# A spacer tile of 96 instead of 32 bytes at the right end of the on-chip memory of a hybrid decoder layer

## The chip, the cores and the metric

The kernel runs on one core of one Trainium2 chip. The metric is the device time of one execution in microseconds (us), as a median of three runs.

## The reference

One decoder layer on x of 1024 tokens by 1024 channels, in float32, in three steps. Each step normalises its input and scales and shifts it by vectors worked out from a condition c (`w_ada`).

```python
def swiglu(h, w12, w3):
    a, b = jnp.split(h @ w12, 2, axis=-1)
    return (jax.nn.silu(a) * b) @ w3
...
x = x + 0.5 * (1.0 + gate[:, 0, None]) * swiglu(h, ffn1_w12[l], ffn1_w3[l])
...
x = x + (1.0 + gate[:, 1, None]) * token_mix(h, w_in[l], ...)
...
x = x + 0.5 * (1.0 + gate[:, 2, None]) * swiglu(h, ffn2_w12[l], ffn2_w3[l])
```

The inner width of both feed-forward blocks is 2816. `token_mix` runs a differential attention and an mLSTM, four heads each, side by side, and ends in a projection by `w_out`. The two feed-forward blocks do the same arithmetic on different weights.

## The kernel before

**Products.** Every large product is kept at float32 precision by splitting both factors in a high and a low part of type float32r: `mm3` (L196 to L200) issues three matmuls of 128 x 128 weights by 128 x 512 moving elements: high by high (L198), high by low (L199), low by high (L200). In the names of the profile, whi and wlo are the parts of a weight tile, the weights of a matmul; what stands before them (B11h, B22l, S, ghi, glo, k) is its moving operand.

```python
def mm3(self, ps, whi, wlo, xhi, xlo, first, last):
    nc = self.nc
    nc.tensor.matmul(ps, whi, xhi, start=first, stop=False, skip_group_check=True)
    nc.tensor.matmul(ps, whi, xlo, start=False, stop=False, skip_group_check=True)
    nc.tensor.matmul(ps, wlo, xhi, start=False, stop=last, skip_group_check=True)
```

Weights come from memory as wraw (`load_raw`, L175, SP's queue), are split by ScalarE and VectorE (`split_w`, L180; L186, L187), and some are first summed by GpSimd (`wsum`, L190; L193), since `wino` (L225) takes products of 2 x 2 blocks with seven multiplications instead of eight. Its moving operands are B11, B21, B22 and four combinations T1 to T4, whose parts lie in eight groups of slots S0 to S7 (`t_ops`, L412). T1's high part is in S0 and its low part in S2, T2's high part in S7 and its low part in S1; T3 and T4 use S3 to S6.

**Stages.** The start and the first feed-forward block run to about 720 us. The middle (projections, attention, mLSTM) follows, then the output projection (`wo_half`, 8 row tiles x 2 halves x 2 parts x 12 matmuls) and, from about 1390 us, the second feed-forward block (`ffn`, L552). A scheduler orders the instructions when the program is built.

**Memory.** Pools of tiles are stacked in the on-chip memory from both ends: those with `side="right"` from the top downwards, all others from the bottom upwards. Big tiles are multiples of 2048 bytes in each of the 128 partitions, weight slices of 512 bytes. So every matmul operand of a pool begins at the same remainder modulo 512, and a small tile ahead of the pools on one side shifts all of that side. `edge` (L978) is such a tile: it is first on the right, and nothing reads or writes it. In the program as it is built, the remainders of the pools which the text speaks of are these (bytes modulo 512):

| pool (what is in it) | side | before | after the change |
|---|---|---|---|
| wring (weights until the middle's projections end) | left | 384 | 384 |
| hpool (B11, B21, B22, S of the first block) | left | 384 | 384 |
| gpool (ghi, glo), tmp (k) of the first block | left | 384 | 384 |
| b12 (B12, in the start alone) | right | 448 | 384 |
| yda, yml (moving operands of the output projection) | left | 384 | 384 |
| wring2 (weights of the output projection and the second block) | right | 448 | 384 |
| b1 (B11, B21, S0, S1 of the second block) | right | 448 | 384 |
| b2 (B22, S2 to S7 of the second block) | left | 384 | 384 |
| gpool2 (ghi, glo), tmp3 (k) of the second block | left | 384 | 384 |

Of the kernel before, what the change touches and what calls it, by code (L numbers as in the profile page):

```python
# [16 lines left out]
F32 = mybir.dt.float32  # L17
# [8 lines left out]
P = 128  # L26
# [929 lines left out]
def build(tc, yT, **A):  # L956
    nc = tc.nc
    with ExitStack() as es:
# [16 lines left out]
            kw = {"side": side} if side else {}  # L975
            return ph, lambda name, **k: ph.enter_context(tc.tile_pool(name=name, reuse_waits="tile", **{**kw, **k}))

        es.enter_context(tc.tile_pool(name="edge", bufs=1, side="right")).tile([P, 8], F32, name="edge")  # L978

        pps, pspool = stack()  # L980
        L.mmps = pspool("mmps", bufs=7, space=PSUM)
# [115 lines left out]
        def each(j):  # L1097
            while begun:
                L.ada_finish(*begun.pop(0))
            for _ in range(2 if j < 8 else 1):  # L1100
                if rest:
# [3 lines left out]
                                                                   bufs=3 if names[n] == "c" else 1),  # L1105
# [242 lines left out]
```

## Time and profile before

| | us |
|---|---|
| median of 3 runs | 2070.29 (2067.78 to 2075.93) |
| the profiled execution | 2070.71 |
| its span in the profile | 2068.9 |
| TensorE busy | 1940.8 |
| VectorE busy | 1498.0 |
| ScalarE busy | 772.6 |
| GpSimd busy | 535.1 |

Over the span the granted TensorE clock was 0.978 of full speed. Durations in the profile are modelled for matmuls, which overlap: a matmul of 0.39 us begins while the one before it is still in the array. So the pace of the engine is read from starts, or from the number of matmuls in a window; the mean durations serve to compare groups. A window counts a matmul that hangs over its edge.

### The profile page before, as it was taken

How to read it: one execution, taken by the hardware profiler on the slowest of the kernel's cores; microseconds unless marked ns; L12 is line 12 of the kernel's file. 1: busy time of each engine (PE TensorE's matmuls, PEld its weight loads, DVE VectorE, ACT ScalarE, POOL GpSimd, SP SyncE). 2: the span in 40 equal slices, each digit the busy share in tenths (PEclk: the TensorE clock that was granted, in tenths of full speed). 3: DMA queues.
4: the chain of work that ended last, by engine and by line, in shares of the span. 5: the costliest groups of instructions: out<-in, count | busy, mean ns of one | idle time of the engine just before them, and what ended most of it. 6: DMA issues, size and time to landing. Idle time of an engine off the chain costs nothing.

```text
span 2068.9 us, 24523 instructions
## 1 busy us (share of the span) xinstructions
PE 1940.8 (94%) x8814; PEld 1574.6 (76%) x8814; DVE 1498.0 (72%) x2431; ACT 772.6 (37%) x1490; POOL 535.1 (26%) x390
## 2 busy tenths in 40 slices
PE   4889999999999987998898989988999999999999
PEld 3678888888888865876676777866888888888887
DVE  8998888777766689568795986478766555556665
ACT  3522322222332365343444875364222222222232
POOL 4422112121111244345331123135212112121120
PEclk9899999999999998999998999998999999999999
DMA  7253333222221241233329853121111111111113
GB/s 278 77 187 127 123 107 122 92 83 102 87 82 56 97 146 48 92 104 126 129 107 233 169 123 113 62 71 61 62 62 41 61 61 41 51 52 51 51 62 122
DMA packets 83274, 202.81 MB, mean 98 GB/s; under 512 B 9680, under 2 KB 18256, under 8 KB 83152
## 3 DMA queue, kind: packets, MB, share of 16 engines
q1 hardware_dynamic: 77504, 184.93, 26.5%
q0 software_dynamic: 4320, 14.75, 3.5%
q10 hardware_dynamic: 1328, 1.57, 0.2%
q8 instruction: 69, 1.13, 0.2%
q14 instruction: 53, 0.43, 0.1%
HBM read 174.02 MB, written 27.26 MB: 97 GB/s over the span
## 4 chain that ended last, share of the span: by engine, by line
PE 74%; DVE 12%; DMA 7%; issue 3%; ACT 2%; POOL 2%; SPq 0%; DVEq 0%; ACTq 0%; POOLq 0%
PE mm L198 24%; PE mm L200 24%; PE mm L199 24%; DMA ok<-qkd 3%; DVE wlo L187 2%; DVE adaacc L323 1%; POOL sf L193 1%; DVE S L419 1%; DVE cv L720 1%; DMA wraw<-in_w 1%; DMA qkd<-qraw 1%; PE t L801 1%; DMA mv<-mlv 1%; DVE S L428 1%; DMA qkd<-qhi 1%
## 5 line engine op out<-in xcount | busy, mean ns | idle before, releaser
L198 PE MATMUL mm<-S,whi 128*128 128x512 f32 x900 | 356.2, 397 | 8.4 <-DVE vc L228 3.7
L186 ACT CAST whi<-wraw 128x512 fp32r<-128x512 f32 x308 | 190.4, 620 | 453.3 <-PE mm L199 433.0
L199 PE MATMUL mm<-S,whi 128*128 128x512 f32 x900 | 354.9, 395 | 4.6 <-DVE S L428 4.6
L200 PE MATMUL mm<-S,wlo 128*128 128x512 f32 x900 | 352.6, 393 | 1.1 <-DVE wlo L187 1.0
L528 DVE SCALAR_TENSOR_TENSOR x<-mm,gate,x 128x512 f32<-128x512 f32 x368 | 269.5, 745 | 108.3 <-PE mm L200 106.0
L193 POOL TENSOR_TENSOR sf<-wraw 128x512 f32<-128x512 f32 x112 | 168.9, 1508 | 485.4 <-DMA wraw<-in_w 288.1
L186 ACT CAST whi<-sf 128x512 fp32r<-128x512 f32 x224 | 138.1, 620 | 411.8 <-PE mm L199 377.7
L187 DVE TENSOR_TENSOR wlo<-wraw,whi 128x512 fp32r<-128x512 f32 x294 | 223.4, 761 | 86.2 <-ACT whi L186 72.3
L199 PE MATMUL mm<-glo,whi 128*128 128x512 f32 x672 | 263.6, 393 | 0.0
L200 PE MATMUL mm<-ghi,wlo 128*128 128x512 f32 x672 | 262.8, 393 | 0.9 <-DVE wlo L187 0.9
L198 PE MATMUL mm<-ghi,whi 128*128 128x512 f32 x672 | 261.9, 394 | 0.1
L193 POOL TENSOR_TENSOR sf<-wraw,sf 128x512 f32<-128x512 f32 x56 | 86.4, 1543 | 482.5 <-DVE wlo L187 395.5
L198 PEld LDWEIGHTS mm<-S,whi 128*128 128x128 f32 x900 | 170.4, 189 | 49.5 <-DVE vc L228 4.1
L199 PEld LDWEIGHTS mm<-S,whi 128*128 128x128 f32 x900 | 170.2, 189 | 43.3 <-DVE S L428 6.1
L200 PEld LDWEIGHTS mm<-S,wlo 128*128 128x128 f32 x900 | 169.9, 189 | 39.8 <-DVE wlo L187 2.4
L187 DVE TENSOR_TENSOR wlo<-sf,whi 128x512 fp32r<-128x512 f32 x224 | 163.0, 730 | 38.8 <-ACT whi L186 38.5
L200 PEld LDWEIGHTS mm<-ghi,wlo 128*128 128x128 f32 x672 | 126.3, 188 | 30.1 <-DVE wlo L187 1.3
L198 PEld LDWEIGHTS mm<-ghi,whi 128*128 128x128 f32 x672 | 126.1, 188 | 28.7 <-ACT ghi L521 0.6
L199 PEld LDWEIGHTS mm<-glo,whi 128*128 128x128 f32 x672 | 126.3, 188 | 28.4
L228 DVE TENSOR_TENSOR c<-w,mm 128x512 f32<-128x512 f32 x84 | 57.2, 686 | 101.4 <-PE mm L200 101.3
L323 DVE SCALAR_TENSOR_TENSOR adaacc<-adac,cs,adaacc 128x256 f32<-128x256 f32 x196 | 112.2, 572 | 12.1 <-DMA adac<-in_wada 10.9
L193 POOL TENSOR_TENSOR sf<-sf,wraw 128x512 f32<-128x512 f32 x56 | 83.0, 1482 | 112.9 <-DVE wlo L187 110.9
(331 smaller groups left out, 3585.7 us busy)
## 6 DMA issues: line engine op xcount, KB each, us to landing
wraw<-in_w SPq DMA_DIRECT2D x142, 512.0 KB
adac<-in_wada SPq DMA_DIRECT2D x112, 256.0 KB
ok<-qkd POOLq DMA_DIRECT2D x16, 512.0 KB, 13.1
adaraw<-in_wada SPq DMA_DIRECT2D x12, 512.0 KB
wraw<-in_wo SPq DMA_DIRECT2D x12, 512.0 KB
x<-in_xT SPq DMA_DIRECT2D x16, 256.0 KB
xd<-x SPq DMA_DIRECT2D x16, 256.0 KB
wraw<-in_wqk SPq DMA_DIRECT2D x8, 512.0 KB
```

What stands on the lines that cost most here:

```text
L186: nc.scalar.copy(out=hi, in_=raw)
L187: (eng or nc.vector).tensor_tensor(out=lo, in0=raw, in1=hi.bitcast(F32), op=ALU.subtract)
L193: self.nc.gpsimd.tensor_tensor(out=s, in0=a, in1=b, op=op)
L198: nc.tensor.matmul(ps, whi, xhi, start=first, stop=False, skip_group_check=True)
L199: nc.tensor.matmul(ps, whi, xlo, start=False, stop=False, skip_group_check=True)
L200: nc.tensor.matmul(ps, wlo, xhi, start=False, stop=last, skip_group_check=True)
L228: add = lambda o, a, b: nc.vector.tensor_tensor(out=o, in0=a, in1=b, op=ALU.add)
L323: nc.vector.scalar_tensor_tensor(out=acc, in0=raws[k], scalar=self.cs[:, k:k + 1], in1=acc, op0=ALU.mult, op1=ALU.add)
L419: eng.tensor_tensor(out=o, in0=a, in1=b, op=ALU.subtract)
L428: e.tensor_tensor(out=T[n][1], in0=v, in1=T[n][0].bitcast(F32), op=ALU.subtract)
L528: self.nc.vector.scalar_tensor_tensor(out=x, in0=ps, scalar=self.gate[:, g:g + 1], in1=x, op0=ALU.mult, op1=ALU.add)
L720: nc.vector.scalar_tensor_tensor(out=v, in0=u[:, j:j + T], scalar=cw(j), in1=v, op0=ALU.mult, op1=ALU.add)
```

## The change

One line of `build`: the unused tile at the right end of the on-chip memory has 24 float32 elements per partition instead of 8, 96 bytes instead of 32. All pools on the right then lie 64 bytes lower; those on the left stay.

```diff
-        es.enter_context(tc.tile_pool(name="edge", bufs=1, side="right")).tile([P, 8], F32, name="edge")
+        es.enter_context(tc.tile_pool(name="edge", bufs=1, side="right")).tile([P, 24], F32, name="edge")
```

The instructions, and their order on each of the five engines, are the same before and after.

## Rows read from the trace of the kernel before

**Rows 1.** The page: busy time by engine, TensorE and its clock in the 40 slices.

```profile
PE 1940.8 (94%) x8814; PEld 1574.6 (76%) x8814; DVE 1498.0 (72%) x2431; ACT 772.6 (37%) x1490; POOL 535.1 (26%) x390
...
PE   4889999999999987998898989988999999999999
...
PEclk9899999999999998999998999998999999999999
```

**Rows 2.** Three stretches: length, busy us of PE, PEld, DVE, ACT, POOL; clock, DMA share, GB/s.

```profile
300.00:700.00 400.00, 400.00 (x1777) 330.46 (x1776) 297.31 (x502) 113.23 (x189) 74.27 (x52) 1.00 0.26 88
1438.00:2064.70 626.70, 626.70 (x2699) 505.62 (x2699) 378.10 (x551) 171.82 (x287) 109.11 (x77) 1.00 0.18 61
1500.00:2000.00 500.00, 500.00 (x2155) 403.52 (x2154) 294.25 (x428) 136.64 (x229) 90.62 (x64) 1.00 0.15 53
```

**Rows 3.** Longest waits, 1450 us to the end: us in total, times, longest.

```profile
ACT whi L186 <- PE mm L199: 347.0, 152, 5.0
...
POOL sf L193 <- DMA wraw<-in_w: 182.8, 10, 19.2
```

**Rows 4.** The transposes of L331 alone, by stretch: us, PE busy, clock.

```profile
300.00:700.00 400.00, 5.33 (x28) 1.00 0.26 88
```

**Rows 5.** Timeline of TensorE, earlier block: start us, duration, engine, line.

```profile
560.47 0.39 PE L198 MATMUL mm<-ghi,whi 128*128 128x512 f32 x1
...
572.48 0.39 PE L200 MATMUL mm<-ghi,wlo 128*128 128x512 f32 x1
```

**Rows 6.** Timeline of TensorE, later block.

```profile
1699.94 0.39 PE L198 MATMUL mm<-ghi,whi 128*128 128x512 f32 x1
...
1712.77 0.39 PE L199 MATMUL mm<-glo,whi 128*128 128x512 f32 x1
```

**Rows 7.** Groups by form, 1500 to 2000 us: busy us, mean ns, idle before.

```profile
L199 PE MATMUL mm<-glo,whi 128*128 128x512 f32 x259 | 101.9, 394 | 0.0
...
L199 PE MATMUL mm<-B22l,whi 128*128 128x512 f32 x64 | 25.2, 394 | 0.0
...
L199 PE MATMUL mm<-B21l,whi 128*128 128x512 f32 x64 | 24.9, 389 | 0.0
L200 PE MATMUL mm<-B11h,wlo 128*128 128x512 f32 x64 | 24.9, 389 | 0.0
```

**Rows 8.** Groups by form, 300 to 700 us.

```profile
L199 PE MATMUL mm<-glo,whi 128*128 128x512 f32 x208 | 81.0, 389 | 0.0
...
L199 PE MATMUL mm<-B22l,whi 128*128 128x512 f32 x52 | 20.2, 389 | 0.0
```

**Rows 9.** Timeline of TensorE, later block: B11, B21 and B22.

```profile
1533.39 0.39 PE L200 MATMUL mm<-B11h,wlo 128*128 128x512 f32 x1
...
1535.43 0.39 PE L200 MATMUL mm<-B11h,wlo 128*128 128x512 f32 x1
...
1541.22 0.40 PE L198 MATMUL mm<-B21h,whi 128*128 128x512 f32 x1
...
1543.73 0.39 PE L200 MATMUL mm<-B21h,wlo 128*128 128x512 f32 x1
...
1546.76 0.39 PE L198 MATMUL mm<-B22h,whi 128*128 128x512 f32 x1
...
1548.86 0.39 PE L198 MATMUL mm<-B22h,whi 128*128 128x512 f32 x1
```

**Rows 10.** Instructions on tile B12h, 30 to 120 us: duration min/median/max.

```profile
L198 PE MATMUL mm<-B12h,whi x16: 388/394/628, 62.2 to 101.2; 128*128 128x512 f32 x16
```

**Rows 11.** Busy time by engine before the wait-free stretch.

```profile
1254.00:1400.00 146.00, 135.97 (x642) 109.75 (x641) 92.12 (x159) 73.67 (x142) 42.47 (x30) 0.97 0.25 87
1400.00:1438.00 38.00, 32.68 (x124) 25.20 (x123) 31.47 (x40) 16.07 (x30) 23.33 (x12) 0.89 0.16 56
```

**Rows 12.** Timeline of TensorE, later block: inside T2.

```profile
1537.05 0.40 PE L198 MATMUL mm<-S,whi 128*128 128x512 f32 x1
...
1538.23 0.39 PE L200 MATMUL mm<-S,wlo 128*128 128x512 f32 x1
```

## The prediction

> **What bounds the kernel now.** I read the page first: TensorE is busy for 94% of the span, and in the last twelve of the forty slices for nine tenths or more of it, with as much of the clock granted [rows 1]. So I asked for the busy time by stretch. From 1438 us to 2064.7 us, which is the second feed-forward block but for its start, the engine is busy 626.70 us out of 626.70, with 2699 matmuls in it and a granted clock of 1.00, which is 2.4 GHz [rows 2]. Nothing holds it back there but its own pace: ScalarE's casts of the weights wait for TensorE, 347.0 us in all, and from 1450 us on no wait of TensorE stands in the list [rows 3]; VectorE is busy for 378.10 us and ScalarE for 171.82 us of the same stretch [rows 2]. In the middle of the first feed-forward block, 300 to 700 us, the picture is the same: 400.00 us out of 400.00 [rows 2]. Both stretches do the same arithmetic with the same lines, so their paces should agree. They don't.
>
> **The pace in the two stretches.** The later stretch starts 2155 matmuls in 500 us, 232.0 ns each [rows 2]. The earlier one starts 1777 in 400 us, of which 28 are the short transposes of L331 [rows 2, 4]. The long matmuls alone are 1749. If the transposes cost nothing, that is 228.7 ns each; if each costs as much as a long one, 225.1 ns. The timeline settles it between these: from 560.47 to 572.48 us there are 53 starts, 12.01 us, so 226.6 ns [rows 5]; the same product of the later block has 55 starts from 1699.94 to 1712.77 us, 12.83 us, so 233.3 ns [rows 6].
>
> What differs is where the operands lie. In the earlier block weights (whi, wlo) and moving operands come from pools at the left end, all at remainder 384 of 512 bytes. In the later one the weights lie at the right end (448), and so do B11 and B21 and two of the eight S slots; B22, the other slots, ghi, glo, and k lie at the left (384). The groups by form show it operand by operand. The later block's B21l and B11h (with wlo) take 389 ns each, ghi, glo and B22 take 394 [rows 7]; in the earlier block glo and B22 took 389 [rows 8]. The duration is modelled with the pipeline's depth in it, but the 5 ns step is in the starts too: nine starts of B11 from 1533.39 to 1535.43 us are 226.7 ns apart, nine of B22 from 1546.76 to 1548.86 us are 233.3 ns apart, 13 us later at the same clock [rows 9]. There is one case the other way round: B12 lies at the right while the first block's weights lie at the left. Its median is 394 ns too, though the fastest is 388 [rows 10]. So each pair in the trace that disagrees modulo 512 is slow, and each that agrees is not.
>
> **The change part by part.** It adds and removes no instruction, wait or transfer, and the order on all five engines stays. Every right-hand pool moves down by 64 bytes, from remainder 448 to 384. That has three parts.
>
> First, the wait-free stretch from 1438 us on: 2699 matmuls now paced at 232.0 ns or slightly more. (A window counts the matmul that hangs over its edge, which makes the pace 626.70/2698 = 232.3 ns there.) After the change all have equal remainders, so I take the earlier block's pace. The ends are 226.6 ns [rows 5] and 228.7 ns [rows 2, 4]; I take 227.3, because 1749 of those leave 2.5 us for 28 transposes, or 90 ns for a quarter of the columns. The gain is 2698 x (232.3 - 227.3) = 13.5 us, and by the ends 15.4 and 9.7 us. All of it lies on the path, as there is no wait to swallow it.
>
> Second, the output projection and the start of the block, 1254 to 1438 us. The output projection's 384 matmuls (8 row tiles, 2 halves, 2 parts, 12 each) read y at the left with weights from the right, and of the 124 after 1400 us [rows 11] some read B22 or S slots at the left: at most 508 x 6 ns = 3.0 us. TensorE is busy for a good nine tenths of the first 146 us and for 32.68 of the last 38 us [rows 11]; between lie waits for the norm's row sums and for splits. The waits stand behind the projection's own results, so an earlier projection moves them forward; matmuls between two waits gain nothing. I take 1.0 us, about half of the projection's own 384 x 5 ns = 1.9 us; the ends are 0 and 3.0.
>
> Third, B12: 16 matmuls on each of three lines in the start [rows 10], 48 x 5 ns = 0.2 us, taken whole; at worst none.
>
> The rest costs nothing. Products of two right-hand tiles, or two left-hand ones, keep their distance. Transposes of right-hand tiles against the identity change theirs; a step of 5 ns on a hundred of them would be 0.5 us, either way, and I take 0. Rows of the wraw tiles land 64 bytes lower; the DMA engines are busy for 18% of the stretch [rows 2], and what waits for a wraw there is GpSimd, 182.8 us [rows 3], whose sums are themselves ahead of TensorE. That is also what would be late next, and 2% of pace does not reach it.
>
> Sum: 13.5 + 1.0 + 0.2 = 14.7 us off the profiled execution's 2070.7, so **2056.0 us**, 0.7% down. That execution is 0.4 us over the median of the runs shown, 2070.29, so nothing has to be corrected. The ends of the terms give 9.7 + 0 + 0 and 15.4 + 3.0 + 0.2: 2061.0 to 2052.1 us.
>
> **The rivals.** *No change, 2070 us.* In every pair I read, equal remainders and the same end of the memory go together, so the trace cannot tell the remainder from the side. If two far-apart regions are what costs 5 ns (a switch of region between the weight read and the moving read), 64 bytes leave it: 0 of the 14.7 us come. For it: the confounding is complete for these single-pass products. Against it: a cost by region would more naturally be paid in full at each matmul, whereas B12 has single fast ones, 388 ns against the median of 394 [rows 10]. The Trainium skill speaks for no change as well: "TensorE: Matmul & The Clock Gate", in the step-by-step part on what happens when a matmul is issued, says that TensorE has two independent read ports, so that loading the next weights takes no read bandwidth from the running matmul. By that rule addresses would not matter at all and the sum would be 0. The trace disagrees with it as far as it goes: one form of instruction has two paces at one clock.
>
> *Slower, about 2081 us.* The remainder matters, but equal ones are the bad case, and the slow pairs are slow for their mixture. In the later block T2 alternates between a left-hand part (high) and a right-hand one (low), whose remainder equals the weights'. Five intervals of it, from 1537.05 to 1538.23 us, make 236 ns [rows 12], more than the 233.3 of products that lie at the left entirely. At that pace for all 2699 matmuls the stretch grows by 4 ns x 2699 = 10.8 us: 2081.5. The point from which it decides is a pace over 232.3 ns with all remainders equal. Against it stands the whole first block, all equal and 227 ns.
>
> *Half.* Only one of the two readings of a matmul (its own weights, or the next one's being loaded meanwhile) counts, or neighbours keep some of the cost: B21 in the later block, eleven intervals from 1541.22 to 1543.73 us, makes 228.2 ns although its remainders agree [rows 9]. With 229.5 ns the first term is 7.6 us and the time 2062. I count it with the forecast's tail.
>
> **How the numbers follow.** Forecast with its tail 85%, no change 11%, slower 4%. The range takes the forecast's ends with 1 us for what a median of three moves, and the half case with some of what lies between it and no change: 2051 to 2066 us; what it leaves out is no change, slower, and a few per cent beyond. Half a per cent, 10.35 us, is about what a measurement of this kernel can tell from no change, so faster by more means under 2059.9 us. Of the 85% that is 77, the other 8 and no change lie within it: 0.77, 0.19, 0.04.
>
> **What would show it.** In the changed kernel's profile the later block's groups ghi, glo and B22 should read 389 ns in place of 394, the window of 500 us should hold about 2200 matmuls instead of 2155, B12's median should fall to 388 or 389, and the first block's groups should stay as they are. The time of the first 1250 us should not move by more than a microsecond. I am wrong if ghi and glo stay at 394, if a wait appears on TensorE after 1440 us, or if the pace falls and the end does not come earlier.

## The result, and the profile after

| | before | changed |
|---|---|---|
| median of 4 runs, us | 2073.11 (2067.78 to 2076.14) | 2052.16 (2045.78 to 2052.71) |
| ratio, with its 95% interval | | 0.9895 (0.9863 to 0.9926) |
| the profiled execution, us | 2070.71 | 2052.71 |

The change makes the kernel 1.05% faster. The two profiled executions lie 18.0 us apart. The page of the changed kernel, its span and its busy times, beside [rows 1]:

```profile
span 2050.9 us, 24523 instructions
...
PE 1921.5 (94%) x8814; PEld 1574.3 (77%) x8814; DVE 1496.5 (73%) x2431; ACT 772.4 (38%) x1490; POOL 532.0 (26%) x390
```

TensorE does the same 8814 matmuls in 19.3 us less busy time. Busy time by stretch, with the columns of [rows 2]:

```profile
300.00:700.00 400.00, 400.00 (x1780) 330.85 (x1779) 297.99 (x503) 113.49 (x190) 72.11 (x52) 1.00 0.25 88
1438.00:2047.00 609.00, 609.00 (x2687) 504.22 (x2686) 375.23 (x548) 171.18 (x285) 108.21 (x77) 1.00 0.18 61
1500.00:2000.00 500.00, 500.00 (x2207) 414.15 (x2207) 306.10 (x445) 141.75 (x237) 95.83 (x68) 1.00 0.16 54
```

The first block is as before (1780 for 1777 matmuls in 400 us). In the later block 500 us now hold 2207 matmuls instead of 2155 (about 2200 were forecast), and TensorE still never waits there. The groups by form of that window, beside [rows 7]:

```profile
L199 PE MATMUL mm<-glo,whi 128*128 128x512 f32 x272 | 105.6, 389 | 0.0
...
L200 PE MATMUL mm<-B11h,wlo 128*128 128x512 f32 x68 | 26.5, 389 | 0.0
...
L199 PE MATMUL mm<-B21l,whi 128*128 128x512 f32 x64 | 24.9, 389 | 0.0
...
L199 PE MATMUL mm<-B22l,whi 128*128 128x512 f32 x64 | 24.9, 389 | 0.0
```

All forms read 389 ns, on whichever side the moving operand lies; ghi, glo and B22 had 394. So the step is gone exactly where it was.

Where the time came from, by the same matmul in both timelines (they issue the same matmuls in the same order):

| matmul | start before, us | start after, us | difference |
|---|---|---|---|
| first of the output projection | 1253.92 | 1254.56 | +0.64 |
| first of the wait-free stretch after the change | 1441.39 | 1438.36 | -3.03 |
| last | 2064.71 | 2046.76 | -17.95 |

From the second to the third row there are 2684 intervals: 623.32 us before (232.24 ns each) and 608.40 us after (226.68 ns each), 14.9 us. The output projection and the block's start give 3.7 us: 1.9 of them come up to the projection's last matmul, 1.7 behind it. All before them gives nothing.

The stretch ahead of the wait-free one, beside [rows 11]:

```profile
1254.00:1400.00 146.00, 135.69 (x653) 111.57 (x652) 92.95 (x164) 75.51 (x145) 42.80 (x30) 0.98 0.25 87
1400.00:1438.00 38.00, 31.18 (x131) 23.75 (x130) 32.94 (x41) 15.56 (x29) 24.13 (x12) 1.00 0.20 69
```

From 1400 to 1438 us the granted clock is 1.00 where it was 0.89 in the execution before: TensorE ran part of those 38 us at 1.2 GHz then. The stretch holds waits in both executions, so what it gives cannot be put down to the change alone.

### The profile page after: what moved, and what is told of

The parts are those of the page before. It is cut to its first block, busy times and chain, and to the rows that moved or that the text cites. A ratio compares the mean times of both kernels' runs of the same rounds, so it can differ in the third digit from the quotient of the medians.

```text
span 2050.9 us, 24523 instructions
## 1 busy us (share of the span) xinstructions
PE 1921.5 (94%) x8814; PEld 1574.3 (77%) x8814; DVE 1496.5 (73%) x2431; ACT 772.4 (38%) x1490; POOL 532.0 (26%) x390
## 4 chain that ended last, share of the span: by engine, by line
PE 75%; DVE 12%; DMA 6%; ACT 3%; issue 3%; POOL 1%; SPq 0%; DVEq 0%; ACTq 0%; POOLq 0%
PE mm L198 24%; PE mm L200 23%; PE mm L199 23%; DMA ok<-qkd 3%; DVE wlo L187 2%; DVE adaacc L323 1%; DVE S L419 1%; DVE S L428 1%; DVE cv L720 1%; PE t L801 1%; POOL sf L193 1%; DMA qkd<-qraw 1%; DVE nm L778 1%; DMA wraw<-in_w 1%; ACT S L379 0%
## 5 line engine op out<-in xcount | busy, mean ns | idle before, releaser
L198 PE MATMUL mm<-S,whi 128*128 128x512 f32 x900 | 354.2, 394 | 7.8 <-ACT whi L186 2.4
L199 PE MATMUL mm<-S,whi 128*128 128x512 f32 x900 | 352.7, 392 | 4.7 <-DVE S L428 4.7
L200 PE MATMUL mm<-S,wlo 128*128 128x512 f32 x900 | 351.5, 392 | 1.5 <-DVE wlo L187 1.4
L199 PE MATMUL mm<-glo,whi 128*128 128x512 f32 x672 | 261.8, 390 | 0.0
L200 PE MATMUL mm<-ghi,wlo 128*128 128x512 f32 x672 | 260.8, 391 | 0.8 <-DVE wlo L187 0.8
L198 PE MATMUL mm<-ghi,whi 128*128 128x512 f32 x672 | 260.0, 391 | 0.1
L198 PEld LDWEIGHTS mm<-S,whi 128*128 128x128 f32 x900 | 170.3, 189 | 46.6 <-ACT whi L186 3.3
L199 PEld LDWEIGHTS mm<-S,whi 128*128 128x128 f32 x900 | 170.2, 189 | 41.9 <-DVE S L428 6.2
L200 PEld LDWEIGHTS mm<-S,wlo 128*128 128x128 f32 x900 | 170.0, 189 | 38.4 <-DVE wlo L187 3.2
L200 PEld LDWEIGHTS mm<-ghi,wlo 128*128 128x128 f32 x672 | 126.4, 188 | 27.4 <-DVE wlo L187 1.2
L198 PEld LDWEIGHTS mm<-ghi,whi 128*128 128x128 f32 x672 | 126.4, 188 | 26.3 <-ACT ghi L521 0.6
L199 PEld LDWEIGHTS mm<-glo,whi 128*128 128x128 f32 x672 | 126.5, 188 | 26.0
```

## The experiments

Two theories stand. By the **remainder theory** the pace of these matmuls is set by the distance of the moving operand's address from the weights', modulo something. By the **side theory** it is set by whether both lie at the same end of the memory, and 64 bytes helped by some other road. "Distance" below is moving operand minus weights, modulo 512 bytes.

**left64: the same agreement by shifting the other side.** Against the changed kernel:

```diff
-...side="right")).tile([P, 24], F32, name="edge")
+...side="right")).tile([P, 8], F32, name="edge")
+        es.enter_context(tc.tile_pool(name="ledge", bufs=1)).tile([P, 16], F32, name="ledge")
```

> The spacer at the right end stays at 32 bytes as in the kernel before, and an unused tile of 64 bytes is put ahead of the pools at the left instead: both sides are then at remainder 448. The output is the reference's. Remainder theory (difference alone): as the changed kernel, about 2052 us, second block at 226.7 ns. If it was the address 384 itself that helped the right-hand side: second block at 233 ns, about 2070 us. Side theory: no gain, 2070 us.

Measured: 2051.42 us, median of 4, beside 2069.81 of the kernel before on that chip; ratio 0.9906 (0.9876 to 0.9937). Its two stretches, with the columns of [rows 2]:

```profile
300.00:700.00 400.00, 400.00 (x1779) 330.66 (x1778) 298.30 (x504) 114.33 (x191) 73.33 (x52) 1.00 0.26 88
1500.00:2000.00 500.00, 500.00 (x2208) 414.15 (x2207) 305.29 (x444) 141.47 (x237) 95.73 (x68) 1.00 0.16 54
```

2208 matmuls in 500 us. Equal remainders bring the gain, be they 384 or 448; the address itself does not matter. A no-change rival that rests on the side is out, since here too the weights stay at the right and ghi, glo and B22 at the left.

**scan1 and scan2: all distances in steps of 32 bytes, all at the left.** One spacer (an unused tile) between each two groups of moving operands in the first block; to make room, the low weight parts have three buffers there (the lines for that are left out here, as in the next four runs).

```diff
-        L.place((4, 3), "B22", "B11", (7, 1), (0, 2), "B21", (5, 6))
+        for i, (n, pad) in enumerate(zip(((), (4, 3), "B22", "B11", (7, 1), (0, 2), "B21", (5, 6)),
+                                         (0, 32, 32, 64, 64, 64, 64, 64))):
+            L.place(n)
+            if pad:
+                hp.tile([P, pad // 4], F32, name=f"pad{i}")
```

scan2 has `(96, 64, 64, 64, 64, 64, 32, 32)`.

> The changed kernel with spacers between the operand groups of the left-hand pool of the first feed-forward block, so that moving operands lie above the remainder of the weights by: T4 0, B22 32, B11 64, T2 128, T1 192, B21 256, T3 320, ghi, glo and k 384 bytes (modulo 512). Weights and moving operands are all at the left. To make room the low weight parts have three buffers instead of four in that block. The output is the reference's. Remainder theory: in the first block T4 stays at 227 ns from start to start, B11 (64) rises to about 232 to 233; the others are not known, and a group further off than 64 bytes is at 233 or more. Side theory: all groups stay at 227, since nothing crosses sides. In the second block everything is at 227 by both. If all else rises to 233, the kernel should take about 10 to 20 us more than the changed one.

> As scan1 with other distances: T4 96, B22 160, B11 224, T2 288, T1 352, B21 416, T3 448, ghi, glo and k 480 bytes. Remainder theory: T3 (448, that of most pairs of the kernel before) at 233 ns, none at 227. Side theory: all at 227. A third theory, that equal remainders are only by chance better than 448 and another distance is better still, expects one of the fifteen groups that are not equal under 226.6 ns; the floor is 213.3 ns, 512 columns at 2.4 GHz.

Measured, in one execution each: 2075.9 and 2082.3 us. The first block and, unchanged, the second, scan1:

```profile
300.00:700.00 400.00, 400.00 (x1744) 324.26 (x1743) 293.20 (x486) 110.80 (x186) 70.96 (x52) 1.00 0.25 85
1500.00:2000.00 500.00, 500.00 (x2207) 414.01 (x2207) 298.60 (x438) 141.15 (x237) 92.72 (x66) 1.00 0.16 54
```

and scan2:

```profile
300.00:700.00 400.00, 400.00 (x1731) 321.84 (x1730) 289.19 (x483) 109.52 (x183) 68.19 (x51) 1.00 0.25 85
1500.00:2000.00 500.00, 500.00 (x2208) 414.15 (x2207) 302.15 (x440) 139.63 (x233) 95.06 (x68) 1.00 0.16 54
```

1744 and 1731 matmuls in 400 us, where the changed kernel has 1780. By distance, the mean interval from start to start, worked out from the timelines from 200 to 710 us (intervals from the seventh matmul of a group on, those over 300 ns, which are waits, left out; 56 to 637 of each):

| distance | 0 | 32 | 64 | 96 | 128 | 160 | 192 | 224 |
|---|---|---|---|---|---|---|---|---|
| ns | 227.4 | 232.9 | 228.9 | 233.7 | 233.1 | 234.6 | 233.5 | 233.3 |

| distance | 256 | 288 | 320 | 352 | 384 | 416 | 448 | 480 |
|---|---|---|---|---|---|---|---|---|
| ns | 228.3 | 233.3 | 228.9 | 233.7 | 232.9 | 233.8 | 233.6 | 233.3 |

Operands on one side pay as well, so the side theory is out a second time. No distance is better than 0. The expectation that 64 would stand at 232 to 233, and everything further off at 233 or more, missed: 64 reads 228.9, 256 reads 228.3 and 320 reads 228.9. The two rows of the table look alike, which says that the remainder might count modulo 256. scan1 takes 23.7 us more than the changed kernel, over the 10 to 20 expected; scan2 30.1; by u0 below, the missing fourth buffer is part of that.

**u0, u448, u256, u64: one distance throughout the first half.** A single spacer ahead of the left-hand operands, so that no product differs from its neighbour; u0 is the control with the three buffers and no spacer.

```diff
+        hp.tile([P, 112], F32, name="pad")
         L.place((4, 3), "B22", "B11", (7, 1), (0, 2), "B21", (5, 6))
```

(112 elements in u448, 64 in u256, 16 in u64.)

> Control for the next three: the changed kernel with three buffers instead of four for the low weight parts up to the output projection, no spacer. The output is the reference's. By every theory: first block at 227 ns from start to start, total 2050 to 2056 us.

> u0 with a spacer of 448 bytes between weights and moving operands at the left, so that every product of the first feed-forward block and of the projections behind it has moving operands at 448 above its weights (modulo 512), the distance that the second block had in the kernel before, without any change of distance from product to product. The output is the reference's. Remainder theory: first block settles at 233.3 ns as in the later block before; 2500 matmuls there x 6.6 ns = 16 us over u0, and up to 11 us more from the 1660 matmuls of the projections. Side theory: as u0.

> The same with 256 bytes. In scan1 the group at 256 settled towards 227 ns after some ten matmuls, and 320 looked like 64, 384 like 128. If the remainder counts modulo 256: 226.7 ns, total as u0 within 3 us. If it counts modulo 512: 230 to 233 ns, 8 to 27 us over u0.

> The same with 64 bytes, moving operands above the weights. If the size of the distance counts, whatever its sign: 233 ns as 448 (64 below). If the sign counts, as scan1's group suggests, where two of three intervals settled at 229.8 and one at 226.4: 228.7 ns, 5 to 9 us over u0.

Measured, one execution each: 2062.3, 2083.5, 2066.2 and 2073.6 us. TensorE from 300 to 640 us (length, busy us and matmuls, clock, DMA), and the first and last row of the timeline of a piece of 82 matmuls on ghi and glo, of u0:

```profile
300.00:640.00 340.00, 339.35 (x1509) 1.00 0.27 92
```

```profile
509.18 0.39 PE L200 MATMUL mm<-ghi,wlo 128*128 128x512 f32 x1
...
527.54 0.39 PE L200 MATMUL mm<-ghi,wlo 128*128 128x512 f32 x1
```

of u448:

```profile
300.00:640.00 340.00, 339.86 (x1473) 1.00 0.27 90
```

```profile
516.44 0.39 PE L200 MATMUL mm<-ghi,wlo 128*128 128x512 f32 x1
...
535.33 0.40 PE L200 MATMUL mm<-ghi,wlo 128*128 128x512 f32 x1
```

of u256:

```profile
300.00:640.00 340.00, 339.90 (x1512) 1.00 0.27 92
```

```profile
511.37 0.39 PE L200 MATMUL mm<-ghi,wlo 128*128 128x512 f32 x1
...
529.72 0.39 PE L200 MATMUL mm<-ghi,wlo 128*128 128x512 f32 x1
```

and of u64:

```profile
300.00:640.00 340.00, 339.97 (x1501) 1.00 0.27 92
```

```profile
511.23 0.39 PE L200 MATMUL mm<-ghi,wlo 128*128 128x512 f32 x1
...
529.77 0.39 PE L200 MATMUL mm<-ghi,wlo 128*128 128x512 f32 x1
```

Over the 81 intervals: u0 18.36 us, 226.7 ns; u448 18.89 us, 233.2 ns; u256 18.35 us, 226.5 ns; u64 18.54 us, 228.9 ns. So the distance that the later block had before costs 6.5 ns also where nothing crosses sides, and the kernel with it takes 21.2 us more than its control, inside the 16 to 27 expected; 14 of them are lost by 739 us, about the end of the first block. (The paces carry the argument here, the totals less so: seven runs of the kernel before lie between 2064.44 and 2077.27 us.) 256 bytes cost nothing in the pace: the remainder counts modulo 256, and agreement modulo 512 is more than is needed. The sign counts too: 64 above costs a third of what 64 below (448) does. Against u0, u64 lost 11.2 us, over the 5 to 9 expected: 4.1 by the end of the first block, and 4.4 of the rest between the same matmuls (1059 and 1137 us in u0) where u256, whose pace is u0's, lost 3.9; so that part is not shown to come from the distance. u256's own 3.9 us, over the 3 expected, come there as well, for it stood 0.6 us ahead of u0 at 1059 us; one execution each cannot tell that from chance. The control missed its 2050 to 2056 us by 6: with three buffers the kernel seems to lose more than I thought.

**wlo64, then p0, plo448 and phi448: which of a matmul's readings pays.** wlo64 put the low weight parts of the second half into a pool of their own, 64 bytes lower, with three buffers.

```diff
...
+        xpool("lopad", bufs=1).tile([P, 16], F32, name="lopad")
+        L.wlop = xpool("wlop", bufs=3)
+        xpool("lopad2", bufs=1).tile([P, 112], F32, name="lopad2")
```

> The changed kernel, with the low weight parts of the second half (output projection and second feed-forward block) in a pool of their own at remainder 320, three buffers instead of four; high parts and moving operands stay at 384. So of the three matmuls of a triple only L200 has weights that disagree. The output is the reference's. If a matmul pays for its own weights: the interval from L200's start to the next one is long (233 ns), the two others 227. If the running matmul is slowed by the weights that are loaded meanwhile for the next: the interval from L199's start to L200's is long. Either way a third of the cost, 5 us over the changed kernel.

Measured: 2077.9 us, 26 over the changed kernel instead of 5. Against it, 13.4 us were lost by the start of the wait-free stretch, 4.6 of them ahead of the output projection, where both kernels do the same, and 11.8 us over the 2684 intervals from there on, 4.4 ns each:

```profile
1500.00:2000.00 500.00, 500.00 (x2166) 406.66 (x2165) 306.94 (x431) 137.43 (x231) 88.20 (x65) 1.00 0.15 53
```

With three buffers the scheduler put some products in another order (high parts ahead, low ones late), so the run is no clean answer. Of the triples (the three matmuls of one `mm3`) 613 still run in order and without waits from 1500 to 2000 us; their intervals are 229.4, 230.7 and 233.5 ns from the starts of L198, L199 and L200, 231.2 in the mean. So the matmul with the disagreeing weights is the longest and its neighbours pay too. And its distance is 64 here, which costs 2.2 ns when every pair has it (u64): one pair out of step among agreeing ones cost 4.4 in the mean, more than all of them out of step alike. (Three buffers alone leave the pace at 226.7, by u0.) The question was asked again in the first block, with four buffers and the order of the triples kept.

```diff
-        lo = self.wring.tile([P, 4, P], F32R, tag="wlo", name="wlo")
+        lo = self.wp.tile([P, 4, P], F32R, tag="wlo", name="wlo", bufs=4)
...
+        pw, wpool = stack("right")
+        L.wp = wpool("wp", bufs=4)
...
```

The pool lies at the right, ahead of all others; spacers of 32 and 64 bytes around it set its remainder in plo448, and phi448 has the high parts in it instead.

> Control for the next two: up to the end of the first feed-forward block the low weight parts lie in a pool at the right end, at remainder 384 like everything else; four buffers as in the changed kernel. The output is the reference's. Remainder theory: first block settles at 226.7 ns on all three lines of a triple, although the low weights are at the other side. Side theory: L200, or the line before it, at 233.

> As p0 with that pool at remainder 448: in the first block only L200's weights disagree with the moving operands (448). The output is the reference's. Intervals from start to start in triples that run in order L198, L199, L200: if a matmul pays for its own weights, the interval from L200's start is 233 ns or more and the other two 227; if the matmul that runs while the next weights are loaded pays, it is the interval from L199's start; if the pace has to settle anew at each change of distance, as after a spacer in the scans, all three are over 227 and their mean is near 231.

> The reverse: the high weight parts (L198, L199) in the pool at 448, the low ones with the rest at 384. The output is the reference's. Own weights: the intervals from L198 and L199 long, from L200 227. Next weights: the intervals from L200 and L198 long, from L199 227. Settling anew: all three over 227, mean 231 to 233.

Measured, one execution each: 2060.6, 2067.3 and 2071.9 us. TensorE from 300 to 640 us in p0:

```profile
300.00:640.00 340.00, 340.00 (x1514) 1.00 0.27 94
```

in plo448:

```profile
300.00:640.00 340.00, 340.00 (x1487) 1.00 0.27 95
```

and in phi448:

```profile
300.00:640.00 340.00, 340.00 (x1474) 1.00 0.27 92
```

The mean intervals by line, from the timelines (200 to 640 us, triples in order and without waits, 567 to 600 intervals of each line):

| interval from the start of | L198, ns | L199, ns | L200, ns | mean, ns |
|---|---|---|---|---|
| p0, all equal | 226.7 | 226.7 | 226.6 | 226.7 |
| plo448, low weights disagree | 228.4 | 229.1 | 235.8 | 231.1 |
| phi448, high weights disagree | 234.2 | 231.3 | 234.6 | 233.3 |

p0 is the third witness against the side theory: its low weights lie at the other end of the memory and cost nothing. (Its 8 us over the changed kernel arise behind the first block; from 788 us on the order of its matmuls is another.) Three theories had been put down: a matmul pays for its own weights, it pays for the next ones, or the pace settles anew at each change of distance. In plo448 the matmul with the disagreeing weights pays most, 9 ns, and its two neighbours 2 ns each, though they agree; the mean is the 231 that the third theory expected. In phi448 it is the lines around L199 that pay most, as the second theory would have it, and the mean is as if all three disagreed. Neither of the first two theories fits both runs; the third gave both means (231, and 231 to 233), but does not say why the lines differ. What stands is the price: one disagreeing matmul of three costs 4.4 of the 6.6 ns, two of three cost them all. Why an address distance costs time at all, and whether two readings collide, stays open.

**The price at the lower clock.** Where the granted clock is 0.5 (1.2 GHz), the distance costs nothing. Six starts of u448 in such a stretch, at distance 448:

```profile
806.69 0.63 PE L198 MATMUL mm<-B22h,whi 128*128 128x512 f32 x1
...
808.82 0.57 PE L200 MATMUL mm<-B22h,wlo 128*128 128x512 f32 x1
```

That is 426 ns each. Between the first block and the output projection the timeline of u448 has 41 intervals of 426 to 427 ns at this clock, and that of u0, where all agree, has 38 of the same length.

## Why the prediction was right

**The pace.** Right, and for the reason given: the distance of the operands, not the side. The first term was 13.5 us, and the two executions show 14.9. The step that was a little off is the pace taken for after, 227.3 ns: it came from a window of the first block that also held 14 intervals of 314 ns, each right behind a pair of the short transposes. The lower end, 226.6 ns from the timeline [rows 5], was the true value, since the later block waits for nothing.

**The output projection and the block's start** are the term that was mis-sized: 1.0 us, with 3.0 as its end, where the executions show 3.7. Two steps failed. The first is to take the projection at half of its 1.9 us, because it holds waits: it gave the 1.9 whole. TensorE waits there for 2.8 us before and 2.9 after; the rest are matmuls close behind each other, and the intervals of those fell from 233.2 to 227.7 ns. The second is the clock, which the term put at nothing. From 1369 to 1441 us, before, changed and left64:

```profile
1369.00:1441.00 72.00, 59.45 (x231) 46.20 (x230) 57.12 (x77) 37.80 (x66) 39.33 (x23) 0.88 0.20 66
```

```profile
1369.00:1441.00 72.00, 57.77 (x238) 44.91 (x237) 57.73 (x78) 37.77 (x66) 39.47 (x22) 0.95 0.20 69
```

```profile
1369.00:1441.00 72.00, 59.50 (x232) 46.90 (x232) 54.60 (x75) 35.59 (x61) 38.26 (x22) 0.88 0.21 73
```

left64 has the agreement too, but the clock of the kernel before, and from the projection's last matmul to the wait-free stretch it gained 0.3 us where the changed kernel gained 1.7. As far as three executions can say, 1.4 of the 3.7 us are the clock of this execution, which is luck. (In the projection left64 gained the same 1.9.)

**B12** was right in kind and too large in size. I said that its median would fall from 394 ns to 388 or 389. On L200 it did, before and changed:

```profile
L200 PE MATMUL mm<-B12h,wlo x16: 388/394/628, 68.7 to 101.6; 128*128 128x512 f32 x16
```

```profile
L200 PE MATMUL mm<-B12h,wlo x16: 388/389/628, 69.2 to 102.0; 128*128 128x512 f32 x16
```

On L198 it stayed in the changed kernel's execution and fell in left64:

```profile
L198 PE MATMUL mm<-B12h,whi x16: 389/394/628, 62.8 to 101.6; 128*128 128x512 f32 x16
```

```profile
L198 PE MATMUL mm<-B12h,whi x16: 389/389/628, 62.3 to 101.1; 128*128 128x512 f32 x16
```

The starts say it directly: eight matmuls on B12 from 98.63 us on are 231.7 ns apart before, eight from 99.09 us on 226.6 ns in the changed kernel. What hides it on L198 in this execution are four intervals of 263 to 339 ns from 75 to 77 us, and the slow ones behind them. The size was too large: the 31 intervals at full clock average 230.0 ns before and 226.8 in left64 (34 of them), 3.2 ns and not 5, and the rest ran at 1.2 GHz, where the distance costs nothing. That leaves 0.1 us, less than what the waits of the start move. (B12 lay 64 above its weights, the distance that u64 shows to be cheaper.)

That a wait lengthens the intervals behind it, whatever the distance, is seen in the changed kernel, where everything agrees, after the last wait of the block's start:

```profile
1438.36 0.39 PE L198 MATMUL mm<-B22h,whi 128*128 128x512 f32 x1
...
1439.52 0.39 PE L200 MATMUL mm<-B22h,wlo 128*128 128x512 f32 x1
...
1441.56 0.39 PE L200 MATMUL mm<-S,wlo 128*128 128x512 f32 x1
```

Five intervals from 1438.36 to 1439.52 us make 232 ns, the nine after them 226.7. Over the whole execution, behind waits and at full clock, the first six intervals average 232, 233, 232, 228, 230 and 230 ns, and the tenth to the twentieth 226.6 to 227.1 (87 to 95 of each of the first ten). What I used against the no-change rival, B12's single fast matmuls, proved nothing: scan1's group at 64, all on one side, has a fast interval (226.9 ns) in three too. The right evidence was in B11 beside B22 [rows 9], and it was confounded with the side until left64, u448 and p0.

**The rivals.** *No change*: each of those three runs speaks against it. The rule of the Trainium skill beside it ("TensorE: Matmul & The Clock Gate", the step-by-step part: two independent read ports) was taken in the prediction to mean that addresses do not matter, and that does not hold here: u0 and u448 differ in 448 bytes of spacer, and in 226.7 against 233.2 ns. Whether it is the weight load that slows the running matmul, which the page denies, no run here shows. *Slower*: equal remainders are the best case, together with 256. Its remark on mixtures has something to it, for in wlo64 a mixture of 0 and 64 cost more than 64 throughout; but u448 is slow without any. *Half*: neighbours do keep some of the cost (plo448, and B21 before [rows 9]), but after the change no neighbour disagrees, so all of it went.

**The numbers.** 2056.0 us was forecast and 2052.16 measured, inside 2051 to 2066. Against the profiled execution the gain was forecast as 14.7 us and is 18.0; 1.4 us of the difference are the pace and 2.7 the projection and the block's start, of which about 1.4 are the clock. B12's 0.2 cannot be seen, since everything ahead of the projection is 0.6 us later.

## What to carry to other kernels

Where TensorE never waits at full clock, count its starts: two stretches of the same work with different paces at one clock mean something that no list of waits shows, and the operands' addresses belong to what may differ. For float32r products of this shape (128 x 128 by 128 x 512) put weights and moving operands at the same remainder modulo 256 bytes in every stage; a spacer does it, and one pair out of step in three lost two thirds of the gain here. Other types and shapes were not tried. Look again whenever a small tile is added to either end, and settle by shifting the other side whether it is the distance or the place.

## What the runs showed that was not expected

- The distance counts modulo 256, and not evenly: 64 above costs 2.2 ns, 64 below 6.5, 128 and every odd multiple of 32 about 6 to 8 ns. At 1.2 GHz the price of 448 is gone (426 to 427 ns, u448 as u0).
- A pace takes time to settle, after a wait as after a change of distance: five intervals of 232 ns ahead of the 226.7 in the changed kernel itself, and 231, 233, 231, 229, 228 and 228 ns in scan1's group at distance 0, with 226.6 to 226.9 from the tenth on.
- At the best distance a matmul still takes 226.7 ns at 2.4 GHz, where half of the 426 to 427 ns at 1.2 GHz would be 213.3. What the other 13 ns are was not tried.
- With one of four buffers for the low weights taken away up to the output projection, the last matmul came 9.6 us later (u0 against the changed kernel, one execution of each).
